# Third sums of the first chunk by accumulating transfers, wide products in the fourth f, and five smaller edits in a hybrid encoder layer

## The chip, the cores and the metric

The kernel runs on one core of one Trainium2 chip. A core has a matrix engine (TensorE, PE in the profile), a vector engine (VectorE, DVE), a scalar engine (ScalarE, ACT), a general engine (GpSimd, POOL) and a queueing engine (SyncE, SP). Each takes its instructions in order. In this kernel SP issues plain transfers and POOL issues transfers that add to what lies at their destination. The metric is device time in microseconds of one execution: 2027.13 us, the median of three runs from 2026.53 to 2027.21.

## The reference, cut to what matters

All in fp32, one layer, 512 tokens, width 2048, 44 groups ("f") of 128 hidden columns.

```python
def reference(x, ...):
    xn = rms_norm(x, attn_norm_g)
    u_val, u_gate, q, k, v = split(xn @ w_in)
    y_conv = conformer_conv(u_val, u_gate, ...)   # GLU, conv of width 31, LayerNorm over channels, swish
    y_na   = neighborhood_attention(q, k, v, rpb)
    mixed  = concat(rms_norm(y_conv, conv_out_g), rms_norm(y_na, na_out_g))
    x  = x + mixed @ w_out
    up = depthwise_conv(rms_norm(x, ffn_norm_g) @ w_up, ...)   # width 3
    gate, val = split(up)
    x  = x + (silu(gate) * val) @ w_down
    return rms_norm(x, final_norm_g)
```

## The kernel before, in words

**Weights.** Every fp32 product is three products of a faster type (fp32r). A unit of weights, 128 x 1024 values or 512 KB, is loaded by SP into one of `NR` = 7 buffers (`raw` or `ws`). `parts` (L113) lets ACT copy it to a rounded high half `whi` (L116) and lets DVE subtract that from the unit, which gives the low half `wlo` (L117). `mm3` (L124) then multiplies high by high, high by low and low by high. There are `NW` = 4 buffers of each half. `weights()` (L148) hands out the next unit of a list and asks for the units up to `AHEAD` = 3 further on, so that what makes a unit is placed some products ahead of its use.

**Order.** The code is written stage by stage. Statistics and other side work are generators that `tick` (L135) advances after a product; `tc.issue_after` lets their instructions start behind a given instruction. A scheduler then fixes one order per engine from the order written, the priorities and the buffers; instructions under `pin` keep program order.

**Stages.** First, until about 488 us, is the input projection: the convolution's columns, the values, queries and keys, with convolution, attention and their statistics between. `stats1` (L283) sums the squares of the input for the first norm, each sum a square by ACT and an addition by DVE (L170); a reduction over partitions is done by PE (L190). `group_a` (L382) computes mean and variance of the convolution's eight results `ys`: it adds them up, and one fp32 matmul with a matrix of ones (L390) sums over the channels. Then the output projection runs in two halves (`out_half`, L572), each of 16 products `po2` of which PSUM bank "mm" (three of them) takes one; `read_a` adds them to `x2` once the norm `ra` is there (L596). A bank "po" of its own serves statistics and attention.

**FFN.** Chunks of `CH` = 4 f's follow, 11 in all. For one f the up projection has four blocks of weights, A11, A21, A22 and A12, and is computed by seven products over sums of blocks. `factors(f)` (L666) makes the seven factors: c=0 is A22, c=1 is the sum A22 + A21 in the buffer `ws`, c=2 is A21 + A11 in the buffer of A21, c=3 is A11, c=4 is `ws` + A11, c=5 is A12, c=6 is `ws` + A12. For f of the first chunk `sums()` (L672) loads A22 a second time by SP into `ws` (L674) and lets POOL accumulate A21 (L675) and, into the buffer of A21, A11 (L677). The third and fourth sums, and all sums of later f's, are DVE additions (L691, L693, L698, L702). A factor's high and low halves are made from the sum, so ACT and DVE wait for it.

**Products.** `up` (L733) computes a factor's product in a "wide" form: eight matmuls of 128x512 (L743), which take high by high and high by low at once, and eight of 128x256 (L749). A factor with even c also opens the next one's bank with one wide matmul. ACT copies results from PSUM (L775) and DVE combines the seven products (L790 to L814). `up_apart` (L818) uses three matmuls of 128x256 instead (L127 to L129) and needs fewer additions (L850 to L856). `hidden` (L869) takes `up_apart` for f=3 and `up` otherwise; f=0 has its own call. `gated_tile` scales by the norm (L873, L874), convolves (L863 to L865), and multiplies (L877). From the second chunk on, the down products `pd` of the chunk before go between the up products, and POOL adds each result to the running sum in HBM (L898).

**Opening.** DVE sets a tile `warm` to one (L102), and PE multiplies it six times by itself (L231), five times 512 columns and once 256, before the first real product.

Of the kernel before, what the change touches and what calls it, by code (L numbers as in the profile page):

```python
# [31 lines left out]
NC_ = CONV // P  # L32
NP_ = HEADS // 2
NF = FF // P
U = 8
# [5 lines left out]
H = S // 2  # L41
LT = S - P
CH = 4
# [23 lines left out]
def layer(ctx: ExitStack, tc: tile.TileContext, xT, xG, xw, w_a, w_in, w_v, w_out, w_up, w_down, par, tab, g3, out, last_out):  # L67
    nc = tc.nc
# [5 lines left out]
    psm = ctx.enter_context(tc.tile_pool(name="psm", bufs=3, space=bass.MemoryType.PSUM))  # L74
    psa = ctx.enter_context(tc.tile_pool(name="psa", bufs=1, space=bass.MemoryType.PSUM))
# [9 lines left out]
    def t2(name, dt=F32):  # L85
        return tp.tile([P, S], dt, tag="t2k", name=name)

    def t4(shape, name):

        return wpool.tile(shape, F32, tag="raw", name=name, bufs=NR)  # L90

    pin = tc.keep_in_program_order
# [5 lines left out]
        o = POFF[name] + i  # L98
        return prm[:, o:o + 1]

    warm = t2("warm", F32R)
    pin(nc.vector.memset(warm.bitcast(F32), 1.0))  # L102
    ones_r = consts.tile([P, P], F32R, name="ones")
    ones = ones_r.bitcast(F32)
    nc.vector.memset(ones, 1.0)
# [3 lines left out]
    def raw_unit(src, n):  # L109
        raw = t4([P, U * P], "raw")  # L110
        return raw, nc.sync.dma_start(raw[:, :n], src)

    def parts(raw, n):  # L113
        hi = wpool.tile([P, U * P], F32R, tag="whi", name="whi", bufs=NW)
        lo = wpool.tile([P, U * P], F32R, tag="wlo", name="wlo", bufs=NW)
        i = nc.scalar.activation(hi[:, :n], raw[:, :n], AF.Copy)  # L116
        j = nc.vector.tensor_sub(lo[:, :n], raw[:, :n], hi[:, :n].bitcast(F32))  # L117
        return hi, lo, i, j

    def unit(src, n):  # L120

        return parts(raw_unit(src, n)[0], n)[:2]

    def mm3(ps, w, wk, mh, ml, start, stop):  # L124
        hi, lo = w[:2]
# [20 lines left out]
    plan, made = [], []  # L146
# [17 lines left out]
    def sum_sq(acc, src, first, to=slice(0, S)):  # L164
        if first:
            nc.scalar.activation(acc, src, AF.Square)
        else:
            q = t2("sq")[:, to]
            nc.scalar.activation(q, src, AF.Square)
            nc.vector.tensor_add(acc, acc, q)  # L170
# [45 lines left out]
    xs, x1 = [], []  # L216
    acc1 = t2("acc1")
# [9 lines left out]
    idle = consts.tile([P, 1], F32, name="idle")  # L227
    pin(nc.scalar.activation(idle, ones[:, 0:1], AF.Square))
    ps = psa.tile([P, 2, S], F32, tag="sc", name="idle")
    for n in 5 * (S,) + (H,):  # L230
        pin(nc.tensor.matmul(ps[:, 0, :n], warm[:, :P], warm[:, :n], start=True, stop=True))  # L231

    for k in range(KD):
        if k < CH:
            raw = t4([P, U * P], "raw")
            n = S + 2 * P + (0 if k else KD)
# [3 lines left out]
        else:  # L240
            if k % CH == 0:
                raw = t4([P, U * P], "raw")
            if k % CH == 0 or k == CH + 2:
                o, n = 2 * (k % CH) * P, 2 * (2 if k < 2 * CH else CH) * P
# [3 lines left out]
        h, l = t2("xh", F32R), t2("xl", F32R)  # L248
# [18 lines left out]
    for step in ORDER:  # L267
# [5 lines left out]
        i = next(a_ if step == "a" else q_)  # L273
# [9 lines left out]
    def stats1():  # L283
        yield
        for k in range(CH, KD):
            sum_sq(acc1, x1[k], False)
            if k % 4 == 3:
                yield
        for _ in range(STAT_AT):
            yield  # L290
        rstd.append((yield from rsqrt_steps(acc1, D, "rstd1", by_token=rtok)))

    steps.append(stats1())

    def project(n):
# [55 lines left out]
    ys, ypair = [], []  # L351
# [6 lines left out]
    def gated(i, pg, pv):  # L358
        g = t2("gate")
        nc.vector.tensor_mul(g, pg, rstd[0])  # L360
        nc.scalar.activation(g, g, AF.Sigmoid)
        nc.vector.tensor_mul(g, g, rstd[0])
        h = t2("ch")
        by = "p (g r c) -> p r g c"
        nc.vector.tensor_mul(h.rearrange("p (r g c) -> p r g c", r=WH, g=NG), pv.rearrange(by, r=WH, g=NG),
                             g.rearrange(by, r=WH, g=NG))
        with shifted(600):

            if i % 2 == 0:
                ypair.append(t4([P, 2, S], "y"))  # L370
            y = ypair[-1][:, i % 2]
            o = POFF["dww"] + i * CK
            nc.vector.tensor_scalar(y, h, prm[:, o + PAD:o + PAD + 1], pc("dwb", i), op0=ALU.mult, op1=ALU.add)
            for j in range(CK):
                if j != PAD:
                    a, b = max(PAD - j, 0), S + min(PAD - j, 0)
                    nc.vector.scalar_tensor_tensor(y[:, a:b], h[:, a + j - PAD:b + j - PAD], prm[:, o + j:o + j + 1],  # L377
                                                   y[:, a:b], op0=ALU.mult, op1=ALU.add)
            ys.append(y)

    ma, ra = [], []

    def group_a():
        acc = t2("acc")
        nc.vector.tensor_add(acc, ys[0], ys[1])
        for i in range(2, NC_):
            nc.vector.tensor_add(acc, acc, ys[i])
        yield
        ps = psa.tile([P, S], F32, tag="po", name="st")
        nc.tensor.matmul(ps, ones, acc, start=True, stop=True)  # L390
        mu = t2("mu")
        nc.vector.tensor_scalar(mu, ps, 1.0 / CONV, None, op0=ALU.mult)
        acc = t2("acc")
        for i in range(NC_):
            nc.vector.tensor_sub(ys[i], ys[i], mu)
            sum_sq(acc, ys[i], i == 0)
            if i == NC_ // 2 - 1:
                yield
        yield
        yield  # L400
        r = yield from rsqrt_steps(acc, CONV, "rln")
        acc = t2("acc")
        for i in range(NC_):
            nc.vector.tensor_mul(ys[i], ys[i], r)
            nc.scalar.activation(ys[i], ys[i], AF.Silu, scale=pc("lng", i), bias=pc("lnb", i))
            ma.append(split(ys[i], pc("cog", i), "ma"))
            sum_sq(acc, ys[i], i == 0)
            if i % 2:
                yield
        yield  # L410
        yield
        ra.append((yield from rsqrt_steps(acc, CONV, "ra")))
# [132 lines left out]
    p, n = -1, 0  # L545
# [26 lines left out]
    def out_half(m, read):  # L572
        for d in range(KD):
            w = weights()
            ps = psm.tile([P, S], F32, tag="mm", name="po2")
            for k in range(U):
                i = mm3(ps, w, k, m[k][0], m[k][1], k == 0, k == U - 1)
            tick(i)
            read(d, ps)
# [86 lines left out]
    def factors(f):  # L666

        def load(q):
            a[q] = raw_unit(w_up[f, q], U * P)[0]
            return a[q]  # L670

        def sums():  # L672
            a["s"] = t4([P, U * P], "ws")
            nc.sync.dma_start(a["s"], w_up[f, A22])  # L674
            nc.gpsimd.dma_start(a["s"], w_up[f, A21], accum_op=ALU.add)  # L675
            load(A21)
            nc.gpsimd.dma_start(a[A21], w_up[f, A11], accum_op=ALU.add)  # L677

        def make(c):
            if c == 0:  # L680
                load(A22)
                if f < CH:
                    sums()
                return a[A22]
            if c == 1 and f < CH:
                load(A11)
            elif c == 2 and f < CH:
                return a[A21]
            elif c == 1:
                a["s"] = t4([P, U * P], "ws")  # L690
                add(a["s"], load(A21), a[A22])  # L691
            elif c == 2:
                add(a[A21], a[A21], load(A11))  # L693
                return a[A21]
            elif c == 3:
                return a[A11]
            elif c == 4:
                add(a["s"], a["s"], a[A11])  # L698
            elif c == 5:
                return load(A12)  # L700
            else:
                add(a["s"], a["s"], a[A12])  # L702
            return a["s"]

        a = {}
        return [lambda c=c: parts(make(c), U * P)[:2] for c in range(7)]

    A11, A21, A22, A12 = range(4)
    add = nc.vector.tensor_add
# [157 lines left out]
        return y  # L867

    def hidden(f, between):  # L869
        return gated_tile(f, *(up_apart if f == CH - 1 else up)(f, between))  # L870

    def gated_tile(f, g, v):
        nc.vector.tensor_mul(g, g, rstd2[0])  # L873
        nc.vector.tensor_mul(v, v, rstd2[0])  # L874
        g, v = conv3(g, f), conv3(v, NF + f)
        nc.scalar.activation(g, g, AF.Silu)
        nc.vector.tensor_mul(g, g, v)  # L877
        return g
# [50 lines left out]
    n = CH  # L929
# [46 lines left out]
    acc = t2("acc3")  # L976
    for d in range(KD):
        ps = psm.tile([P, S], F32, tag="mm", name="pd")[:, fm]
# [8 lines left out]
    sums, v, r, y, w = (sm.tile([P, CH], F32, tag="rs" + c, name="rs" + c) for c in "lvryw")  # L987
    v, r, y, w = (t[:, :1] for t in (v, r, y, w))
# [129 lines left out]
```

## Time and profile before

| | us |
|---|---|
| median of three runs | 2027.13 |
| the profiled execution | 2026.74 |
| its span | 2024.9 |
| PE busy | 2012.7 (99%) |
| DVE busy | 1670.3 (82%) |
| ACT busy | 1051.5 (52%) |
| POOL busy | 166.5 (8%) |

In a row of a timeline the first number is the start in us from the span's beginning, the second the time, then come engine, line, operation, result, inputs and shape; "x3" means three merged instructions, and a bracket at the end says how long the engine was idle before and what ended it. The time of one matmul is longer than the distance between two, since they are pipelined; distances between starts count. In a row of windows come the bounds, the length, the busy time of PE, its weight loads, DVE, ACT and POOL, each with its instructions, and then PE's granted clock, the mean share of the 16 DMA engines, and GB/s. A row of transfers gives size and median time from issue to landing.

### The profile page before, as it was taken

The numbers are of one execution on the slowest core, as the hardware profiler recorded it, in microseconds if no ns is written. First come the engines' busy times: TensorE is split into PE (matmuls) and PEld (weight loads), VectorE is DVE, ScalarE is ACT, GpSimd is POOL, SyncE is SP. The second block draws the span as 40 slices with busy tenths as digits, with TensorE's granted clock in tenths as the row PEclk, the third lists the DMA queues.
The fourth block names the chain that finished last, engine by engine and source line by source line (L and its number), as shares of the span: only waits on it lengthen the run. The fifth ranks groups of instructions, "written<-read, shape, count | busy, mean of one in ns | idle before, by whom it ended". The sixth has DMA issues, their size and how long they took to land.

```text
span 2024.9 us, 28118 instructions
## 1 busy us (share of the span) xinstructions
PE 2012.7 (99%) x10546; PEld 1719.8 (85%) x10546; DVE 1670.3 (82%) x2302; ACT 1051.5 (52%) x1685; POOL 166.5 (8%) x196
## 2 busy tenths in 40 slices
PE   9999999999999999999999999999999999999998
PEld 7888888888888898888888888888888888888887
DVE  7986888988576899888888888888888888879875
ACT  6323344466346655555555555555555555555563
POOL 0000000000002101111111111111111111110111
PEclk9999999999999999999999999999999999999999
DMA  7232333336348745566565565565566565564683
GB/s 256 84 105 85 115 95 111 106 127 215 106 121 208 195 132 146 126 146 146 125 146 146 132 139 146 130 141 146 121 150 146 125 146 146 127 144 126 146 202 131
DMA packets 98503, 282.68 MB, mean 140 GB/s; under 512 B 10944, under 2 KB 12224, under 8 KB 98368
## 3 DMA queue, kind: packets, MB, share of 16 engines
q1 hardware_dynamic: 72000, 230.55, 37.2%
q0 software_dynamic: 26368, 50.34, 16.8%
q8 instruction: 83, 1.36, 0.3%
q14 instruction: 52, 0.43, 0.1%
HBM read 226.32 MB, written 54.53 MB: 139 GB/s over the span
## 4 chain that ended last, share of the span: by engine, by line
PE 96%; DVE 2%; DMA 1%; ACT 1%; issue 0%; SPq 0%; ACTq 0%; DVEq 0%
PE pu L743 26%; PE pu L749 14%; PE pd L129 8%; PE pd L127 8%; PE pd L128 8%; PE pj L127 5%; PE pj L129 5%; PE pj L128 5%; PE po L127 3%; PE po L128 3%; PE po L129 3%; PE pv L324 1%; PE pv L323 1%; PE pv L325 1%; PE trp L497 1%; PE po L512 1%
## 5 line engine op out<-in xcount | busy, mean ns | idle before, releaser
L116 ACT ACTIVATE whi<-raw 128x1024 fp32r<-128x1024 f32 x364 | 384.4, 1058 | 504.9 <-PE pj L128 139.7
L117 DVE TENSOR_TENSOR wlo<-raw,whi 128x1024 fp32r<-128x1024 f32 x364 | 444.8, 1223 | 211.8 <-ACT whi L116 202.9
L743 PE MATMUL pu<-xc,whi 128*128 128x512 f32 x2352 | 580.7, 391 | 0.6 <-DVE uu L797 0.3
L743 PEld LDWEIGHTS pu<-xc,whi 128*128 128x128 f32 x2352 | 433.7, 188 | 83.7 <-issue 0.7
L749 PEld LDWEIGHTS pu<-xc,wlo 128*128 128x128 f32 x2352 | 307.2, 191 | 14.7
L749 PE MATMUL pu<-xc,wlo 128*128 128x256 f32 x2352 | 311.9, 283 | 0.0
L129 PE MATMUL pd<-hh,wlo 128*128 128x512 f32 x640 | 250.7, 392 | 0.7 <-DVE wlo L117 0.7
L127 PE MATMUL pd<-hh,whi 128*128 128x512 f32 x640 | 250.1, 391 | 0.0
L128 PE MATMUL pd<-hl,whi 128*128 128x512 f32 x640 | 249.5, 390 | 0.0
L898 POOL DMA_DIRECT2D x2d<-pdc x160 | 139.3, 872 | 1119.5 <-ACT pdc L897 892.2
L127 PE MATMUL pj<-xh,whi 128*128 128x512 f32 x512 | 199.2, 394 | 0.5 <-DVE xh L253 0.5
L129 PE MATMUL pj<-xh,wlo 128*128 128x512 f32 x512 | 199.0, 391 | 0.2 <-DVE wlo L117 0.2
L128 PE MATMUL pj<-xl,whi 128*128 128x512 f32 x512 | 199.2, 392 | 0.0
L775 ACT ACTIVATE pl<-pu 128x256 f32<-128x256 f32 x294 | 109.7, 381 | 151.3 <-PE pu L743 144.3
L377 DVE SCALAR_TENSOR_TENSOR y<-ch,prm,y 128x501 f32<-128x501 f32 (+14 forms) x240 | 173.7, 743 | 4.3
L116 ACT ACTIVATE whi<-ws 128x1024 fp32r<-128x1024 f32 x132 | 139.7, 1058 | 69.7 <-PE pu L743 55.1
L117 DVE TENSOR_TENSOR wlo<-ws,whi 128x1024 fp32r<-128x1024 f32 x132 | 161.3, 1222 | 14.4 <-ACT whi L116 14.0
L129 PEld LDWEIGHTS pd<-hh,wlo 128*128 128x128 f32 x640 | 120.2, 188 | 29.6 <-DVE wlo L117 4.4
L128 PEld LDWEIGHTS pd<-hl,whi 128*128 128x128 f32 x640 | 120.3, 188 | 24.6
L127 PEld LDWEIGHTS pd<-hh,whi 128*128 128x128 f32 x640 | 120.5, 188 | 22.6
L897 ACT ACTIVATE pdc<-pd 128x512 f32<-128x512 f32 x160 | 93.9, 588 | 80.6 <-PE pd L129 67.4
L127 PEld LDWEIGHTS pj<-xh,whi 128*128 128x128 f32 x512 | 96.5, 189 | 21.2 <-ACT whi L223 1.0
(216 smaller groups left out, 2728.8 us busy)
## 6 DMA issues: line engine op xcount, KB each, us to landing
raw<-in_w_up SPq DMA_DIRECT2D x176, 512.0 KB, 3.8
raw<-in_w_down SPq DMA_DIRECT2D x88, 512.0 KB, 4.0
x2d<-pdc POOLq DMA_DIRECT2D x160, 256.0 KB, 4.9
raw<-in_w_in SPq DMA_DIRECT2D x60, 512.0 KB, 3.7
raw<-in_w_out SPq DMA_DIRECT2D x32, 512.0 KB, 3.8
raw<-in_w_v SPq DMA_DIRECT2D x16, 512.0 KB, 3.7
tab<-in_tab SPq DMA_DIRECT2D x32, 256.0 KB, 5.2
x<-in_xT SPq DMA_DIRECT2D x16, 256.0 KB, 5.5
```

Source lines behind the costliest of these rows:

```text
L116: i = nc.scalar.activation(hi[:, :n], raw[:, :n], AF.Copy)
L117: j = nc.vector.tensor_sub(lo[:, :n], raw[:, :n], hi[:, :n].bitcast(F32))
L127: nc.tensor.matmul(ps, hi[:, a], mh, start=start, stop=False)
L128: nc.tensor.matmul(ps, hi[:, a], ml, start=False, stop=False)
L129: return nc.tensor.matmul(ps, lo[:, a], mh, start=False, stop=stop)
L323: nc.tensor.matmul(ps, xh, wh[:, f], start=kk == 0, stop=False)
L377: nc.vector.scalar_tensor_tensor(y[:, a:b], h[:, a + j - PAD:b + j - PAD], prm[:, o + j:o + j + 1], y[:, a:b], op0=ALU.mult, op1=ALU.add)
L743: i = nc.tensor.matmul(ps, w[0][:, k * P:(k + 1) * P], comb[c][k], start=k == 0, stop=stop and k == ks[-1])
L749: i = nc.tensor.matmul(ps[:, H:], w[1][:, k * P:(k + 1) * P], comb[c][k][:, :H], start=False, stop=stop and k == U - 1)
L775: nc.scalar.activation(to, ps, AF.Copy)
L897: nc.scalar.activation(t, ps, AF.Copy)
L898: nc.gpsimd.dma_start(xd[d], t, accum_op=ALU.add)
```

## The change

1. The tile `warm` has 256 columns and is set by POOL; PE multiplies it 16 times with 256 columns.
2. The squares that `stats1` adds are issued behind the low half of the first unit.
3. The results `ys` are added up as each is made. `group_a` splits the sum into a high and a low half (one ACT copy, one DVE subtraction) and sums each over the channels by an fp32r matmul.
4. The product `po2` number 3 of the first half goes to the bank "po".
5. The fifth f (f=4) makes its first two sums as the first chunk does: one more load by SP, two accumulating transfers by POOL, no DVE additions L691 and L693.
6. For f=0 to 3 the third sum, `ws` + A11, is an accumulating transfer from HBM by POOL, in place of the DVE addition L698. On POOL's queue the four new transfers stand as follows: that of f=0 after the fourteenth of the sixteen L624 accumulates of the second norm; that of f=1 between L675 and L677 of f=2; that of f=2 between L675 and L677 of f=3; that of f=3 after L677 of f=3. The two of f=4 follow.
7. f=3 uses `up` instead of `up_apart`.

```diff
-    warm = t2("warm", F32R)
-    pin(nc.vector.memset(warm.bitcast(F32), 1.0))
+    warm = t2("warm", F32R)[:, :H]
+    pin(nc.gpsimd.memset(warm.bitcast(F32), 1.0))
...
-    for n in 5 * (S,) + (H,):
-        pin(nc.tensor.matmul(ps[:, 0, :n], warm[:, :P], warm[:, :n], start=True, stop=True))
+    for _ in range(16):
+        pin(nc.tensor.matmul(ps[:, 0, :H], warm[:, :P], warm, start=True, stop=True))
...
         for k in range(CH, KD):
-            sum_sq(acc1, x1[k], False)
+            with tc.issue_after(made[0][3].ins):
+                sum_sq(acc1, x1[k], False)
...
             ys.append(y)
+            if i == 1:
+                ysum.append(t2("ysum"))
+            if i:
+                nc.vector.tensor_add(ysum[0], ysum[0] if i > 1 else ys[0], y)
...
     def group_a():
-        acc = t2("acc")
-        nc.vector.tensor_add(acc, ys[0], ys[1])
-        for i in range(2, NC_):
-            nc.vector.tensor_add(acc, acc, ys[i])
+        h, l = t2("yh", F32R), t2("yl", F32R)
+        nc.scalar.activation(h, ysum[0], AF.Copy)
+        nc.vector.tensor_sub(l, ysum[0], h.bitcast(F32))
         yield
         ps = psa.tile([P, S], F32, tag="po", name="st")
-        nc.tensor.matmul(ps, ones, acc, start=True, stop=True)
+        for i, m in enumerate((h, l)):
+            nc.tensor.matmul(ps, ones_r, m, start=i == 0, stop=i == 1)
...
-            ps = psm.tile([P, S], F32, tag="mm", name="po2")
+            ps = (psa.tile([P, S], F32, tag="po", name="po2") if m is ma and d == 3 else
+                  psm.tile([P, S], F32, tag="mm", name="po2"))
...
             if c == 0:
                 load(A22)
-                if f < CH:
+                if f <= CH:
                     sums()
                 return a[A22]
-            if c == 1 and f < CH:
+            if c == 1 and f <= CH:
                 load(A11)
-            elif c == 2 and f < CH:
+            elif c == 2 and f <= CH:
                 return a[A21]
...
+            elif c == 4 and f < CH:
+                nc.gpsimd.dma_start(a["s"], w_up[f, A11], accum_op=ALU.add)
             elif c == 4:
                 add(a["s"], a["s"], a[A11])
...
     def hidden(f, between):
-        return gated_tile(f, *(up_apart if f == CH - 1 else up)(f, between))
+        return gated_tile(f, *up(f, between))
```

`unit` and `factors` also return the whole of what `parts` returns, so that the subtraction can be named in item 2.

More of the change, by code (lines that the diff above doesn't have):

```diff
@@ L120, in unit @@
     def unit(src, n):
-        return parts(raw_unit(src, n)[0], n)[:2]
+        return parts(raw_unit(src, n)[0], n)
     def mm3(ps, w, wk, mh, ml, start, stop):
@@ L379, in gated @@
             ys.append(y)
-    ma, ra = [], []
+            if i == 1:
+                ysum.append(t2("ysum"))
+            if i:
+                nc.vector.tensor_add(ysum[0], ysum[0] if i > 1 else ys[0], y)
+    ma, ra, ysum = [], [], []
     def group_a():
-        acc = t2("acc")
-        nc.vector.tensor_add(acc, ys[0], ys[1])
-        for i in range(2, NC_):
-            nc.vector.tensor_add(acc, acc, ys[i])
+        h, l = t2("yh", F32R), t2("yl", F32R)
+        nc.scalar.activation(h, ysum[0], AF.Copy)
+        nc.vector.tensor_sub(l, ysum[0], h.bitcast(F32))
         yield
         ps = psa.tile([P, S], F32, tag="po", name="st")
-        nc.tensor.matmul(ps, ones, acc, start=True, stop=True)
+        for i, m in enumerate((h, l)):
+            nc.tensor.matmul(ps, ones_r, m, start=i == 0, stop=i == 1)
         mu = t2("mu")
@@ L705, in factors @@
         a = {}
-        return [lambda c=c: parts(make(c), U * P)[:2] for c in range(7)]
+        return [lambda c=c: parts(make(c), U * P) for c in range(7)]
     A11, A21, A22, A12 = range(4)
```

## The prediction

> **What bounds the kernel now.** I read the page's chain first, then the busy time by 25 us windows, then the timeline wherever a window shows TensorE (PE) under 25.00.
>
> ```profile
> span 2024.9 us, 28118 instructions
> PE 96%; DVE 2%; DMA 1%; ACT 1%; issue 0%; SPq 0%; ACTq 0%; DVEq 0%
> ```
> ```profile
> 700.00:725.00 25.00, 24.70 (x142) 21.64 (x141) 24.72 (x37) 16.09 (x27) 1.76 (x2) 1.00 0.57 150
> 750.00:775.00 25.00, 24.26 (x133) 20.82 (x132) 24.95 (x33) 15.94 (x26) 1.76 (x2) 1.00 0.43 114
> ```
>
> PE carries the end. So a gain is either fewer PE cycles or a PE gap closed, and anything else counts only if it makes PE wait. But from 700 to 775, where most of the change lies, VectorE (DVE, the third number after the comma) is as full as PE: 24.72 and 24.95 of 25. What holds DVE up there holds PE up soon after.
>
> The profiled run took 2026.74 us, its span 2024.9, so 1.84 lies around the span. The median of the runs shown is 2027.13, 0.39 above the profiled run; I sum against 2026.74 and add 0.39. Within 0.2% is within 4.05 us of 2027.13, about what a measurement of this kernel can tell from no change.
>
> **The change part by part.**
>
> *Warm-up (memset on POOL, 16 matmuls of 256).*
>
> ```profile
> 1.45 2.72 PE L231 MATMUL idle<-warm 128*128 128x512 f32 x6 [1.45 <-DVE warm L102]
> 4.68 1.19 PE L127 MATMUL pj<-xh,whi 128*128 128x512 f32 x2 [0.51 <-DVE xh L253]
> ```
>
> The six matmuls hold 2816 columns in 2.72 us, so 4096 columns take 2.72 × 4096/2816 = 3.96 us at that rate: from 1.45 to 5.4, 0.7 past the first product's 4.68. That product waits for data, and so do those behind it, so a late start can be made up and a warmer array cannot run ahead. Between +0.7 and a gain of the 0.51 us idle I take 0. The Trainium skill ("TensorE: Matmul & The Clock Gate", Part 1) says about 3.4 us of sustained activity bring full rate; by it the longer filler could end half rate sooner, which would be worth those 0.5 us at most.
>
> *First statistics behind the first low half.*
>
> ```profile
> 25.19 2.28 DVE L170 TENSOR_TENSOR acc<-acc,sq 128x512 f32<-128x512 f32 x3
> 27.39 1.22 DVE L117 TENSOR_TENSOR wlo<-raw,whi 128x1024 fp32r<-128x1024 f32 x1
> ...
> 28.05 0.39 PE L128 MATMUL pj<-xl,whi 128*128 128x512 f32 x1
> 28.66 0.50 PE L129 MATMUL pj<-xh,wlo 128*128 128x512 f32 x1 [0.22 <-DVE wlo L117]
> ```
>
> PE's starts stand 0.61 apart where others stand 0.23 apart: 0.38 lost, because three sums go ahead of the low half (wlo). They move behind it. What is late next is the reduction L190 and the scale after it; I leave 0.1 for that. Gain 0.3 (0 to 0.4).
>
> *Mean of group A.*
>
> ```profile
> 410.46 1.02 PE L390 MATMUL st<-acc,ones 128*128 128x512 f32 x2
> ...
> 411.54 0.39 PE L129 MATMUL pj<-xh,wlo 128*128 128x512 f32 x1
> ```
>
> From 410.46 to 411.54 lie this fp32 matmul and one ordinary one (0.23): it costs 0.85. Two fp32r matmuls of 512 columns cost 2 × 0.23 = 0.45. Gain 0.4. The split adds one ACT copy and one DVE subtraction of 128x512, and seven sums move earlier, all beside projection work; bounds 0.2 to 0.5.
>
> *One output product in another bank.*
>
> ```profile
> 498.70 0.60 ACT L213 ACTIVATE ra<-st 128x512 f32<-128x512 f32 x1 [0.76 <-PE st L207]
> ...
> 499.43 0.39 PE L129 MATMUL po<-mah,wlo 128*128 128x512 f32 x1
> 500.07 0.50 PE L127 MATMUL po<-mah,whi 128*128 128x512 f32 x1 [0.26 <-DVE oa L596]
> ```
>
> PE loses 500.07 − 499.43 − 0.23 = 0.41 waiting for a bank. The "po" bank is free when ACT has read `st`, at 499.30, before it is wanted at 499.66. Gain 0.4 (0 to 0.4).
>
> *Wide products in the fourth f.*
>
> ```profile
> 730.70 0.28 PE L127 MATMUL pu<-xc,whi 128*128 128x256 f32 x1
> ...
> 750.86 2.23 PE L743 MATMUL pu<-xc,whi 128*128 128x512 f32 x9
> 752.93 2.08 PE L749 MATMUL pu<-xc,wlo 128*128 128x256 f32 x16
> 754.84 3.59 PE L743 MATMUL pu<-xc,whi 128*128 128x512 f32 x15
> ```
>
> The fourth f (f=3) holds PE from 730.70 to 750.86, 20.16 us. A wide one has 56 matmuls of 512, (752.93 − 750.86)/9 = 0.230 each, and 56 of 256, 1.91/16 = 0.119 each: 19.5 us. Gain 0.65. On DVE it adds two 128x512 and three 128x256 adds, about 2.2 us, and ACT some copies; ACT has room, DVE hardly.
>
> *Fifth f's two sums by transfers.* DVE loses L693 and L691, an add of the same shape:
>
> ```profile
> 750.39 1.22 DVE L693 TENSOR_TENSOR raw<-raw 128x1024 f32<-128x1024 f32 x1
> 759.78 1.22 DVE L117 TENSOR_TENSOR wlo<-raw,whi 128x1024 fp32r<-128x1024 f32 x1
> ...
> 759.92 0.40 PE L128 MATMUL pd<-hl,whi 128*128 128x512 f32 x1
> 761.06 0.50 PE L129 MATMUL pd<-hh,wlo 128*128 128x512 f32 x1 [0.74 <-DVE wlo L117]
> ```
>
> The 2 × 1.22 us removed about pay for the 2.2 added just before. PE's gap at 761.06 (1.14 − 0.23 = 0.91) hangs on DVE's backlog: between 0 and 0.9 I take a gain of 0.4. The two transfers and one more SP load stand behind f=3's on their queues; with f=3's 20 us of PE work over them, landing times of some 4 to 10 us (rows below) stay hidden. Without that cover each microsecond late would be one of PE's.
>
> *Third sum of the first chunk by transfers.* This decides the sign. For f < 4 the DVE add L698 (`ws += A11`) becomes a POOL accumulate from HBM. POOL issues in order, and for f=1 the new transfer stands behind L675 of f=2 (689.79) and ahead of L677 (691.73).
>
> ```profile
> 689.79 0.90 POOL L675 DMA_DIRECT2D ws<-in_w_up  x1 [17.80 <-DMA ws<-in_w_up]
> 691.73 0.89 POOL L677 DMA_DIRECT2D raw<-in_w_up  x1 [1.04 <-DVE rsy L176]
> ```
> ```profile
> DMA to landing us min/median/max: 5.6/7.2/7.5
> ...
> DMA to landing us min/median/max: 6.2/8.0/10.2
> ```
> ```profile
> raw<-in_w_up SPq DMA_DIRECT2D x176, 512.0 KB, 3.8
> ```
> ```profile
> 699.00:700.00 1.00, 1.00 (x9) 0.92 (x8) 0.69 (x2) 0.47 (x2) 0.00 (x0) 1.00 1.04 279
> ```
> ```profile
> 693.47 1.23 DVE L117 TENSOR_TENSOR wlo<-ws,whi 128x1024 fp32r<-128x1024 f32 x1
> 694.61 1.13 DVE L201 SCALAR_TENSOR_TENSOR dg<-ident,rsy,dg 128x128 fp32r<-128x128 f32 x4
> ...
> 696.32 1.22 DVE L702 TENSOR_TENSOR ws<-ws,raw 128x1024 f32<-128x1024 f32 x1
> ...
> 699.59 1.22 DVE L117 TENSOR_TENSOR wlo<-ws,whi 128x1024 fp32r<-128x1024 f32 x1 [0.31 <-PE pu L749]
> ...
> 702.30 0.75 DVE L864 SCALAR_TENSOR_TENSOR uy<-g,prm,uy 128x511 f32<-128x511 f32 x1 [0.28 <-ACT uy L863]
> ...
> 705.00 0.42 DVE L797 TENSOR_TENSOR uu<-pu,pl 128x256 f32<-128x256 f32 x1
> ...
> 708.37 1.22 DVE L117 TENSOR_TENSOR wlo<-ws,whi 128x1024 fp32r<-128x1024 f32 x1
> ...
> 715.52 1.22 DVE L698 TENSOR_TENSOR ws<-ws,raw 128x1024 f32<-128x1024 f32 x1
> ```
> ```profile
> 705.56 0.47 PE L743 MATMUL pu<-xc,whi 128*128 128x512 f32 x1 [0.30 <-DVE uu L797]
> ```
>
> It is issued at 689.79 + 0.90 = 690.7. The landing times are those of L675 (5.6 to 7.5), of L677 (6.2 to 10.2) and of a plain load of the same size (3.8); the DMA engines are full here (share 1.04). The 10.2 belongs to the transfer issued at 691.73, second behind L675, the nearest row: the new one takes its place. Landing 690.7 + 10.2 = 700.9.
>
> Behind it wait ACT's high half (1.06) and then DVE's low half (693.47 today), in order. Between that low half's start and L797's lie 705.00 − 693.47 = 11.53 us; 1.71 of it (694.61 to 696.32) now goes ahead and about 0.75 is idle time around the marked waits. So L797 starts 11.53 − 1.71 − 0.75 = 9.05 after the low half, which is landing + 1.06 + 9.05. It frees the bank PE waits for at 705.56, already late by 0.30 today. PE's delay is therefore landing + 10.1 − 705.0 = landing − 694.9: 6.0 at 700.9; 1.4 at the fastest accumulate (5.6); none at 3.8 (694.5); 7.5 if it shares the full engines with the transfer behind it.
>
> The Trainium skill ("DMA: Bandwidth & Descriptors", Anatomy of one DMA) puts such a transfer at 2.0 us plus bytes at 436 GB/s, an estimate of 3.2 us here: landing 693.9 and no delay, though the accumulates measured here took twice that or more.
>
> For f=2 the new transfer is issued when DVE has done the low half of 708.37, at 709.6. At 5.6 to 7.5 us it lands at 715.2 to 717.1, is split by ACT until 716.3 to 718.2, and DVE, there at 715.52, idles 0.8 to 2.7 but saves the 1.14 of L698: −0.3 to +1.6. f=3 is alike. Together I take a loss of 0.3, bounds 0 and 3.2. For f=0 the new transfer follows this one on POOL, and its sum is first read here:
>
> ```profile
> 664.36 0.86 POOL L624 DMA_DIRECT2D sq<-sq  x1 [1.24 <-ACT xc L610]
> ```
> ```profile
> 677.13 1.06 ACT L116 ACTIVATE whi<-ws 128x1024 fp32r<-128x1024 f32 x1 [1.79 <-PE pu L128]
> ```
>
> From 665.2 to 677.1 are 11.9 us, over the longest 10.2: nothing. It delays the last two sums of squares of the second norm behind it on POOL's queue, by no more than half its own time on full engines, about 2 us; DVE's idle time in front of that norm may take that in, so 0 to 2, and I take 0.
>
> *Sum.* Gains 0.3 + 0.4 + 0.4 + 0.65 + 0.4 = 2.15; losses 6.0 + 0.3 = 6.3. Net +4.15: 2026.74 + 4.15 + 0.39 = 2031.3. The 10.2 us is the longest of eight such landings, so I shade it by 0.3 and say 2031.0, 0.19% over the median: nominally no change, on its slow edge.
>
> **Rivals.**
>
> *The transfers are hidden.* If f=1's new accumulate lands as a plain load does, by 694.5, nothing waits and the gains stay: 2027.13 − 2.15 = 2025.0. For it: 3.8 us for the same bytes, and L675's smallest 5.6 leaves only 1.4. Against: the full engines after 693, and no accumulate under 5.6. It decides if the landing takes under 4.2 us. Chance 0.20.
>
> *The later f's wait too.* If f=2 and f=3 land like L677's worst, at 10.2 us, each holds DVE up by 709.6 + 10.2 + 1.06 − 715.52 − 1.14 = 4.2 us (nothing up to a landing time of 6.0, then one for one), in a stretch where DVE has nothing to spare: one such adds 4 to the forecast, 2035; both 2039. This is the one that ends on the other side of the bound. For it: DVE at 24.95 of 25 and the wide f=3 adding 2.2. Against: fewer loads run beside them. Chance 0.25.
>
> *The statistics of the second norm come late*, pushed by f=0's transfer: 2 us more, 2033. Chance 0.05.
>
> *More is gained than named*, DVE being freed at the right moments by 4 × 1.14: all gains at their upper bounds with the opening's 0.5 give 0.4 + 0.5 + 0.4 + 0.65 + 0.9 + 0.5 = 3.35, 2023.8, and 2022.7 with L698's 1.14 once more. Chance 0.05.
>
> **How the numbers follow.** My forecast has 0.45, with its own range 2028 to 2033; about 0.25 of it lies within 0.2% and 0.20 above. Hidden: 0.17 within, 0.03 below. The two slower rivals are above, the last below. Faster 0.08, same 0.42, slower 0.50. The range goes from 2024 (hidden, with a little more gained) to 2036 (one later f waiting in full).
>
> **What would show it.** Right: DVE and ACT idle some 6 us before f=1's fifth halves, ended by a DMA into `ws`, and one PE gap of 5 to 7 us shortly after 705; no PE gap at 28.7, 500.1; two short matmuls for `st` near 410; f=3 in 19.5 us. Wrong: that transfer landing under 5 us, or gaps of the same kind at f=2 and f=3, or a PE gap before the first wide product.

## The result and the profile after

The changed kernel takes 2041.77 us (median of six, 2038.56 to 2043.21) against 2026.65 us before (median of six, 2026.3 to 2027.21): ratio 1.0073, 95% interval 1.0062 to 1.0084. It is slower by 15 us, where 2031.0 with a range to 2036 was forecast. The profiled execution took 2043.18 us, near the top of its runs.

The page of the changed kernel, its first lines and its chain:

```profile
span 2041.3 us, 28049 instructions
PE 2018.6 (99%) x10500; PEld 1720.2 (84%) x10500; DVE 1666.2 (82%) x2301; ACT 1052.6 (52%) x1692; POOL 172.0 (8%) x203
...
PE 95%; DVE 2%; DMA 1%; issue 1%; ACT 1%; ACTq 0%; POOL 0%; DVEq 0%; POOLq 0%
```

```profile
75.00:100.00 25.00, 25.00 (x112) 20.72 (x111) 24.86 (x36) 9.88 (x14) 0.00 (x0) 1.00 0.22 64
```
```profile
75.00:100.00 25.00, 22.81 (x95) 18.41 (x95) 24.96 (x35) 8.80 (x12) 0.00 (x0) 0.94 0.28 85
...
700.00:725.00 25.00, 17.40 (x79) 14.68 (x78) 16.42 (x23) 11.56 (x17) 2.62 (x3) 0.80 0.69 165
750.00:775.00 25.00, 23.34 (x131) 19.68 (x129) 23.63 (x33) 16.45 (x26) 0.00 (x0) 1.00 0.59 168
```

The page as a whole hardly differs; the windows show where the time goes. The single row above is the stretch from 75 to 100 in the kernel before, the others are the changed kernel; the rows of before from 700 and from 750 stand at the head of the prediction. PE, the first number after the comma, falls to 17.40 of 25 in the stretch from 700, and to 22.81 in the stretch from 75, where it was full before. In both of these the granted clock (third number from the end) drops too: 0.80 and 0.94. In 700 to 725 DVE falls to 16.42, so PE and DVE wait together.

Line numbers from here on are those of the kernel at hand. In the changed kernel L681 and L683 are the accumulates that were L675 and L677, L704 is the new transfer, L751 and L757 are the wide product's L743 and L749, L783 is the copy L775, and L805 is the addition L797.

The starts of the same matmuls in both timelines give the bill:

| start of | before | after | shift |
|---|---|---|---|
| first `pv`, value projection | 51.53 | 50.81 | −0.72 |
| first `sc`, attention | 236.58 | 239.95 | +3.37 |
| last `pj` of the input projection | 477.35 | 480.25 | +2.90 |
| first `pu`, up projection | 669.14 | 671.54 | +2.40 |
| first `pd`, down products | 759.22 | 773.99 | +14.77 |
| end of the span | 2024.9 | 2041.3 | +16.4 |

Two places lose: 4.1 us at the value projection and 12.4 us in the first chunk, with 1.6 more just behind it.

*The value projection.* Timelines of ACT and PE, first before, then after:

```profile
89.59 1.06 ACT L116 ACTIVATE whi<-raw 128x1024 fp32r<-128x1024 f32 x1 [4.38 <-PE pv L324]
93.21 0.69 ACT L333 ACTIVATE vg<-pv,rsy 128x512 f32<-128x512 f32 x1 [2.56 <-PE pv L325]
...
95.05 0.39 PE L127 MATMUL pj<-xh,whi 128*128 128x512 f32 x1
```
```profile
94.30 1.06 ACT L116 ACTIVATE whi<-raw 128x1024 fp32r<-128x1024 f32 x1 [4.38 <-PE pv L325]
95.27 0.67 ACT L334 ACTIVATE vg<-pv,rsy 128x512 f32<-128x512 f32 x1
95.95 0.68 ACT L337 ACTIVATE vx<-pv,rsy 64x512 f32<-64x512 f32 x1
...
94.11 0.39 PE L326 MATMUL pv<-wlo,xh 128*128 128x512 f32 x1
96.68 0.50 PE L127 MATMUL pj<-xh,whi 128*128 128x512 f32 x1 [2.19 <-ACT vx L337]
...
97.70 0.63 PE L127 MATMUL pj<-xh,whi 128*128 128x512 f32 x1
98.13 0.63 PE L128 MATMUL pj<-xl,whi 128*128 128x512 f32 x1
```

PE's next product needs a bank that ACT frees by `vg` and `vx`. Before, ACT did that at 93.21. After, the high half at 94.30 stands ahead of `vg` in ACT's order; it waits for its own buffer, which the last `pv` products hold until then, and the copies wait behind it. PE stands 2.35 us beyond its pace and then starts matmuls 0.43 apart in place of 0.23 for some 3.4 us; the granted clock is 0.50 between 98 and 100.

*The first chunk, f=1.* POOL's queue, the landing times of the new transfers (L704), ACT, DVE and PE of the changed kernel, with one row of DVE in the kernel before (680.50):

```profile
694.53 0.88 POOL L681 DMA_DIRECT2D ws<-in_w_up  x1 [20.17 <-DMA ws<-in_w_up]
695.16 1.17 POOL L704 DMA_DIRECT2D ws<-in_w_up  x1
```
```profile
DMA to landing us min/median/max: 7.1/7.8/10.5
```
```profile
705.78 1.06 ACT L116 ACTIVATE whi<-ws 128x1024 fp32r<-128x1024 f32 x1 [8.72 <-DMA ws<-in_w_up]
706.74 0.36 ACT L783 ACTIVATE vv<-pu 128x256 f32<-128x256 f32 x1
```
```profile
680.50 0.69 DVE L661 TENSOR_TENSOR acc<-acc,sq 128x512 f32<-128x512 f32 x1
```
```profile
685.61 0.69 DVE L667 TENSOR_TENSOR acc<-acc,sq 128x512 f32<-128x512 f32 x1 [2.63 <-DMA sq<-sq]
...
706.87 1.23 DVE L117 TENSOR_TENSOR wlo<-ws,whi 128x1024 fp32r<-128x1024 f32 x1 [7.96 <-ACT whi L116]
...
716.44 0.42 DVE L805 TENSOR_TENSOR uu<-pu,pl 128x256 f32<-128x256 f32 x1
```
```profile
706.89 2.69 PE L751 MATMUL pu<-xc,whi 128*128 128x512 f32 x8 [1.88 <-ACT whi L116]
709.37 1.91 PE L757 MATMUL pu<-xc,wlo 128*128 128x256 f32 x8
717.00 0.77 PE L751 MATMUL pu<-xc,whi 128*128 128x512 f32 x1 [5.72 <-DVE uu L805]
717.57 1.91 PE L757 MATMUL pu<-xc,wlo 128*128 128x256 f32 x8
719.27 4.12 PE L751 MATMUL pu<-xc,whi 128*128 128x512 f32 x12
```

The transfer is issued behind L681, at 695.16, and lands 10.5 us later, at 705.7. ACT waits 8.72 for it, DVE 7.96, and PE stops twice, by 2.0 and 6.0 us beyond its pace: first for the high half itself, then for the bank that L805 frees. The granted clock is 0.50 from about 715 to 721. Eight 128x256 matmuls then take 1.70 (717.57 to 719.27), against 0.95 at full rate. The row at 685.61 is a second finding: DVE waits 2.63 us for the last sum of squares of the second norm, on which it did not wait before (680.50).

*In f=3 and behind it* (in f=2 PE has no gap of note):

```profile
750.17 1.06 ACT L116 ACTIVATE whi<-ws 128x1024 fp32r<-128x1024 f32 x1 [4.26 <-PE pu L751]
...
751.26 1.22 DVE L117 TENSOR_TENSOR wlo<-ws,whi 128x1024 fp32r<-128x1024 f32 x1 [2.88 <-ACT whi L116]
```
```profile
753.23 0.50 PE L751 MATMUL pu<-xc,whi 128*128 128x512 f32 x1 [1.28 <-ACT pl L783]
...
775.48 0.50 PE L128 MATMUL pd<-hl,whi 128*128 128x512 f32 x1 [0.86 <-DVE hl L891]
...
777.82 0.50 PE L128 MATMUL pd<-hl,whi 128*128 128x512 f32 x1 [0.68 <-DVE hl L891]
```

f=3's transfer was issued at 743.01 and landed at 750.07. The bracket of ACT's row at 750.17 names PE, but the products that held that buffer of `whi` were done at about 746.4; what came at 750.07 is the landing. ACT and DVE stand for it, PE follows with a gap of 1.4, since ACT's copies out of PSUM queue behind the waiting high half, and DVE's lost time comes up again at the first down products, 1.03 + 0.85 beyond pace.

### The profile page after: what moved, and what is told of

Its sections match the earlier page's. It is cut to its first block, busy times and chain, and to the rows that moved or that the text cites. A ratio compares the mean times of both kernels' runs of the same rounds, so it can differ in the third digit from the quotient of the medians.

```text
span 2041.3 us, 28049 instructions
## 1 busy us (share of the span) xinstructions
PE 2018.6 (99%) x10500; PEld 1720.2 (84%) x10500; DVE 1666.2 (82%) x2301; ACT 1052.6 (52%) x1692; POOL 172.0 (8%) x203
## 4 chain that ended last, share of the span: by engine, by line
PE 95%; DVE 2%; DMA 1%; issue 1%; ACT 1%; ACTq 0%; POOL 0%; DVEq 0%; POOLq 0%
PE pu L751 26%; PE pu L757 14%; PE pd L129 8%; PE pd L128 8%; PE pd L127 8%; PE pj L127 6%; PE pj L129 5%; PE pj L128 5%; PE po L127 3%; PE po L128 3%; PE po L129 3%; PE pv L325 1%; PE pv L324 1%; PE pv L326 1%; PE trp L502 1%
## 5 line engine op out<-in xcount | busy, mean ns | idle before, releaser
L117 DVE TENSOR_TENSOR wlo<-raw,whi 128x1024 fp32r<-128x1024 f32 x364 | 444.2, 1221 | 210.7 <-ACT whi L116 203.8
L751 PE MATMUL pu<-xc,whi 128*128 128x512 f32 x2408 | 596.8, 392 | 8.9 <-DVE uu L805 5.7
L751 PEld LDWEIGHTS pu<-xc,whi 128*128 128x128 f32 x2408 | 444.8, 189 | 96.1 <-issue 6.2
L757 PEld LDWEIGHTS pu<-xc,wlo 128*128 128x128 f32 x2408 | 316.1, 192 | 15.1
L757 PE MATMUL pu<-xc,wlo 128*128 128x256 f32 x2408 | 320.7, 283 | 0.0
L128 PE MATMUL pd<-hl,whi 128*128 128x512 f32 x640 | 249.6, 390 | 1.6 <-DVE hl L891 1.5
L129 PE MATMUL pd<-hh,wlo 128*128 128x512 f32 x640 | 250.3, 391 | 0.0
L129 PE MATMUL pj<-xh,wlo 128*128 128x512 f32 x512 | 199.2, 392 | 0.0
L128 PE MATMUL pj<-xl,whi 128*128 128x512 f32 x512 | 198.8, 391 | 0.0
L783 ACT ACTIVATE pl<-pu 128x256 f32<-128x256 f32 x301 | 112.2, 381 | 154.9 <-PE pu L751 147.9
L117 DVE TENSOR_TENSOR wlo<-ws,whi 128x1024 fp32r<-128x1024 f32 x132 | 161.1, 1220 | 27.9 <-ACT whi L116 27.7
L378 DVE SCALAR_TENSOR_TENSOR y<-ch,prm,y 128x500 f32<-128x500 f32 (+14 forms) x240 | 173.5, 740 | 4.3
L129 PEld LDWEIGHTS pd<-hh,wlo 128*128 128x128 f32 x640 | 120.1, 188 | 28.4 <-DVE wlo L117 3.2
L128 PEld LDWEIGHTS pd<-hl,whi 128*128 128x128 f32 x640 | 120.2, 188 | 27.5 <-DVE hl L891 2.9
```

Of the source, the lines that this page charges most:

```text
L128: nc.tensor.matmul(ps, hi[:, a], ml, start=False, stop=False)
L129: return nc.tensor.matmul(ps, lo[:, a], mh, start=False, stop=stop)
L751: i = nc.tensor.matmul(ps, w[0][:, k * P:(k + 1) * P], comb[c][k], start=k == 0, stop=stop and k == ks[-1])
L757: i = nc.tensor.matmul(ps[:, H:], w[1][:, k * P:(k + 1) * P], comb[c][k][:, :H], start=False, stop=stop and k == U - 1)
L783: nc.scalar.activation(to, ps, AF.Copy)
```

## The experiments

Each group of four kernels was timed beside runs of the kernel before: 2026.77 us with the first four, 2027.0 with the next, 2027.09 with the last.

**Third sums by VectorE again.**

```diff
-            elif c == 4 and f < CH:
-                nc.gpsimd.dma_start(a["s"], w_up[f, A11], accum_op=ALU.add)
```

> The changed kernel with the third sum of f=0 to 3 added by VectorE again; everything else of the change stays. Theory A (the new accumulating transfers stop PE in f=1, through the high and low half that wait for the landing): the two gaps of 2.0 and 6.0 us in f=1, the slow clock after them and the 1.4 us gap in f=3 go, some 12 us in all: 2041.8 - 12 = 2030 (2028 to 2032). Rival B (VectorE, loaded by the wide fourth f, is what runs late, and the transfers only show it): VectorE gets 4.6 us more work in the same stretch, so the gaps stay or grow: 2040 or more.

Measured 2027.79 (2026.48 to 2028.49), ratio 1.0001 (0.9993 to 1.0010). Theory A, and more of it than expected: 14.0 us off the changed kernel. Both gaps of f=1, the one in f=3 and those at the down products are gone. The gap at 94 is still there, but this execution shows no slow clock behind it (granted clock 1.00):

```profile
94.03 0.39 PE L326 MATMUL pv<-wlo,xh 128*128 128x512 f32 x1
96.61 0.50 PE L127 MATMUL pj<-xh,whi 128*128 128x512 f32 x1 [2.19 <-ACT vx L337]
96.95 0.39 PE L128 MATMUL pj<-xl,whi 128*128 128x512 f32 x1
97.18 0.40 PE L129 MATMUL pj<-xh,wlo 128*128 128x512 f32 x1
```

The same gap costs 2.5 us here and 4.1 in the other trace. So a stop may or may not take the clock down, and that is one likely cause of the spread of the runs: 2.0 us in this kernel and 0.7 in the version below that has no gap at 94.

**Mean of group A as before.** The seven sums stand in `group_a` again, with one fp32 matmul.

```diff
-            if i == 1:
-                ysum.append(t2("ysum"))
-            if i:
-                nc.vector.tensor_add(ysum[0], ysum[0] if i > 1 else ys[0], y)
...
-        for i, m in enumerate((h, l)):
-            nc.tensor.matmul(ps, ones_r, m, start=i == 0, stop=i == 1)
+        nc.tensor.matmul(ps, ones, acc, start=True, stop=True)
```

> The changed kernel with the mean of group A as before (the seven sums in group_a, one fp32 matmul). Theory A (the seven sums placed early change ACT's order: one more high half goes ahead of the copies that free the value projection's banks, and PE stands 2.35 us and then runs some 3.4 us at half rate): the gap at 94 goes, 4.1 us gained and 0.45 lost at the fp32 matmul: 2041.8 - 3.6 = 2038.2 (2037 to 2039.5). Rival B (the statistics that are put off behind the first low half are what comes late there): the gap stays, 2042.2.

Measured 2038.48 (2037.6 to 2040.78), theory A: no gap at 94, although the first statistics are still put off. The split is undone here too, but the fourth experiment keeps the split and has no gap at 94 either. What moved the high half ahead on ACT is thus the place of seven sums on DVE: with them early, the scheduler that fixes one order per engine chose another order for ACT.

**Third sums by transfers alone, in the kernel before.**

```diff
+            elif c == 4 and f < CH:
+                nc.gpsimd.dma_start(a["s"], w_up[f, A11], accum_op=ALU.add)
             elif c == 4:
```

> The kernel before with one edit alone: the third sum of f=0 to 3 by accumulating transfers. Theory A (this edit alone makes the stop): 2026.7 + 12 = 2038.5 (2036 to 2040.5), with gaps of about 2 and 6 us in f=1. Rival B (it costs what was forecast, 6.3, and the rest of the 12 comes from its meeting with the other edits): 2033.

Measured 2038.25 (2036.67 to 2040.45), 11.5 over the kernel before: theory A. This edit makes the stop without the others' help, and the 6.3 of losses in the forecast were little more than half of it.

**Without both.** The third sums by VectorE, and the split kept while the sums stand where they stood before.

```diff
-            if i == 1:
-                ysum.append(t2("ysum"))
-            if i:
-                nc.vector.tensor_add(ysum[0], ysum[0] if i > 1 else ys[0], y)
...
+        ysum.append(t2("ysum"))
+        nc.vector.tensor_add(ysum[0], ys[0], ys[1])
+        for i in range(2, NC_):
+            nc.vector.tensor_add(ysum[0], ysum[0], ys[i])
         h, l = t2("yh", F32R), t2("yl", F32R)
```

> The changed kernel with the third sums by VectorE again and, for the mean of group A, the split into two fp32r matmuls kept but the seven sums added where they stood before. Theory A (those two places are the whole loss, the other edits gain what their terms say): no gap at 94 nor in f=1; 2041.8 - 12 - 4.1 = 2025.7 (2024.3 to 2027). Rival B (the fifth f's sums and the wide fourth f only move VectorE's backlog to the down products, 1.9 us lost there now against 0.9 before): 2026.5 to 2028, no better than before.

Measured 2030.16 (2028.79 to 2032.43): a miss for both theories. The gap at 94 is gone and the down products show none, but new waits came, in a place neither had named (waits of PE from 420 to 520):

```profile
PE st L190 <- DVE acc L170: 2.1, 2, 1.5
PE st L207 <- ACT ao L523: 1.4, 1, 1.4
PE po L127 <- ACT ra L213: 0.7, 1, 0.7
```

The variance and the attention's norm come late. The seven sums and the split then both stand between the last `y` and the mean. Against the version below that has the late sums without the split (2024.62), the mean comes at 412.54 in place of 411.19, and the last of the eight subtractions of the mean at 431.38 in place of 427.81, with attention work of DVE ahead of it. That this order makes the norms late is a reading of the traces; no run puts the order alone right. The split, then, wants the early sums; what is bad about them is what they do to ACT's order at 94.

**f=1 alone by VectorE.**

```diff
-            elif c == 4 and f < CH:
+            elif c == 4 and f < CH and f != 1:
```

> The changed kernel with the third sum of f=1 alone added by VectorE; those of f=0, 2 and 3 stay accumulating transfers. Theory A (f=1 is special: its transfer goes out between two others of POOL while the DMA engines are full): both gaps of f=1 and the slow clock after them go, about 9.7 us, and the others stay small: 2041.8 - 9.7 = 2032 (2030.5 to 2034). Rival B (any such transfer comes late, the next one then makes the stop): f=2 stops PE by 4 us or more, 2036 or above.

Measured 2034.47 (2032.81 to 2035.93), 7.3 off the changed kernel. That is 0.5 above theory A's range. f=1 is the largest part, but the other three still cost 2034.47 − 2027.79 = 6.7, more than theory A left them. It isn't rival B's stop either: PE loses 0.4 in f=2. The rest is a gap in f=1, which has no transfer of its own now, and the down products again (the last row, 0.3, is there before the change too):

```profile
PE pu L751 <- ACT pl L783: 2.0, 2, 1.8
PE pd L128 <- DVE hl L891: 1.5, 2, 0.9
PE pu L751 <- DVE uu L805: 0.3, 1, 0.3
```

**POOL's queue turned round.** The new transfer of f=1 goes out ahead of the first accumulate of f=2. The same edit names f=4, where it changes nothing: f=3's transfer already stood first there. `third` lists the new transfers.

```diff
-            nc.gpsimd.dma_start(a["s"], w_up[f, A21], accum_op=ALU.add)
+            with tc.issue_after(third[-1].ins) if f in (2, 4) else nullcontext():
+                nc.gpsimd.dma_start(a["s"], w_up[f, A21], accum_op=ALU.add)
...
-                nc.gpsimd.dma_start(a["s"], w_up[f, A11], accum_op=ALU.add)
+                third.append(nc.gpsimd.dma_start(a["s"], w_up[f, A11], accum_op=ALU.add))
```

> The changed kernel with the order of POOL's queue turned round: the new transfer of f=1 is issued before the first accumulate of f=2 (and that of f=3 before those of f=4). Theory A (it is late because it stands behind the other one, first on the queue and then on the DMA engines): it is issued some 1.5 us earlier and lands 5 to 7.5 us after that, near 700 in place of 705.7; PE's stop shrinks by 5 to 7 us: 2035.5 (2034 to 2037.5), while f=2's own sums land later. Rival B (the DMA engines are full anyhow and it lands after 10 us whatever its place): over 2039.

Measured 2035.7 (2032.67 to 2038.12), theory A. Here L707 is the new transfer and L684 the accumulate:

```profile
694.63 0.88 POOL L707 DMA_DIRECT2D ws<-in_w_up  x1 [20.17 <-DVE rsr L174]
695.19 1.23 POOL L684 DMA_DIRECT2D ws<-in_w_up  x1
...
702.73 1.06 ACT L116 ACTIVATE whi<-ws 128x1024 fp32r<-128x1024 f32 x1 [7.81 <-DMA ws<-in_w_up]
```

Issued only 0.5 us earlier, it lands 3.1 us earlier, 8.0 after issue (702.6) in place of 10.5. So its place behind the other accumulate costs 3.1 us of landing time in these two executions, and 6.1 of the run time with what hangs on it; but first in the queue it is still too slow for a use that leaves 4.2: PE's longest stop in f=1 is now 3.0 us.

**Mean and third sums both undone.** The edits of the first two experiments together.

> The changed kernel with the third sums by VectorE and the mean of group A as before, sums and fp32 matmul. Theory A: against the version with the third sums alone undone (2027.8) the gap at 94 goes (4.0 with its slow clock) and the fp32 matmul and the gap before the variance come back (0.45 + 0.3): 2024.5 (2023.8 to 2025.5). Rival B (as with the sums moved back but the split kept, 2030.2, the late statistics take the gain again): 2028 or more.

Measured 2024.62 (2024.4 to 2025.82), ratio 0.9989 (0.9980 to 0.9997): theory A. What is left of the change gains 2.4 us.

**Banks read first.** The sums stay early; the first high half after the first half of the value projection is held behind the copies `vg` and `vx` on ACT. Third sums by VectorE.

```diff
+    hold = []
...
+        if hold:
+            with tc.issue_after(hold.pop().ins):
+                i = nc.scalar.activation(hi[:, :n], raw[:, :n], AF.Copy)
...
+        if half == 0:
+            hold.append(last)
```

Here `last` is the last `vx` copy.

> The changed kernel with the third sums by VectorE and one high half (the first after the first half of the value projection) held back on ACT until the copies that free the value projection's banks are done; the sums stay where the change puts them. Theory A (only that order makes the gap at 94): gap gone, the rest as in the version with the third sums alone undone: 2027.8 - 4.0 = 2023.8 (2023 to 2024.8). Rival B (the high half that is held back is then late itself): a gap of 1 us or more right after the value projection, 2025 or above.

Measured 2024.04 (2023.84 to 2024.56), ratio 0.9985 (0.9976 to 0.9994): theory A, and the fastest version. `vg` starts at 92.74 and the gap at 94 is gone. That one order on ACT was worth 2027.79 − 2024.04 = 3.75 us (4.0 when each is taken against the runs of the kernel before beside it).

**Only f=1 by transfer.**

```diff
-            elif c == 4 and f < CH:
+            elif c == 4 and f == 1:
```

> The changed kernel with the third sum by transfer for f=1 alone; f=0, 2 and 3 by VectorE. Theory A (the four transfers' costs add up: f=1 is worth the 7.3 by which its removal made the changed kernel faster): 2027.8 + 7.3 = 2035.1 (2034 to 2036.3). Rival B (the stop of f=1 covers part of what f=0 costs, so alone it costs more): 2037 or above. Rival C (it costs what was forecast, 6.0 or less, because without the transfer of f=0 the chain of the norm is on time): 2033.8 or below.

Measured 2037.03 (2034.97 to 2039.33): 9.2 over 2027.79, just inside rival B. Its transfer is issued at 694.42 and lands after 11.0 us. Alone it costs more than the 7.3 that its removal gave, so it hides part of another's cost. PE's waits from 680 to 800, in its longest execution:

```profile
PE pu L751 <- DVE uu L805: 7.1, 1, 7.1
PE pu L751 <- ACT whi L116: 2.2, 1, 2.2
```

The down products do not wait here, so that wait belongs to f=2's and f=3's transfers. No run has one of those two alone.

**Only f=0 by transfer.**

```diff
-            elif c == 4 and f < CH:
+            elif c == 4 and f == 0:
```

> The changed kernel with the third sum by transfer for f=0 alone. Theory A (it pushes the last sum of squares of the second norm, VectorE waits 2 us for that, and PE stands for some 2 us in f=1, with a slow clock after it): 2027.8 + 2.5 = 2030.3 (2029.3 to 2031.5). Rival B (VectorE has idle time there that takes it in, as the prediction had it): 2028 (2027 to 2028.8).

Measured 2029.11 (2026.6 to 2032.54): 1.3 over 2027.79, short of theory A's range by 0.2 and beyond rival B's by 0.3, with a wide spread. The mechanism is A's: the wait of 1.8 below is also the one that was left in f=1 when its own transfer was taken out (2.0 above). In the profiled execution, the longest, DVE and PE read:

```profile
686.24 0.69 DVE L667 TENSOR_TENSOR acc<-acc,sq 128x512 f32<-128x512 f32 x1 [3.26 <-DMA sq<-sq]
```
```profile
PE pu L751 <- ACT pl L783: 1.8, 1, 1.8
PE st L190 <- DVE acc L667: 0.9, 1, 0.9
PE pu L751 <- DVE uu L805: 0.3, 1, 0.3
```

**The best version without the wide fourth f,** and **the best version without the fifth f's transfers.**

```diff
-        return gated_tile(f, *up(f, between))
+        return gated_tile(f, *(up_apart if f == CH - 1 else up)(f, between))
```

> The best version so far (third sums by VectorE, value projection's banks read first) with f=3 as before, three 128x256 matmuls. Theory A (the wide form is worth its PE time, 0.65): 2024.0 + 0.65 = 2024.7. Rival B (the 2.2 us that it adds on VectorE come back as a gap, so it is worth nothing): 2024.0 or less.

Measured 2024.23 (2023.98 to 2024.84), so the wide form is worth about 0.2, nearer to rival B; its runs overlap those of the best version.

```diff
-                if f <= CH:
+                if f < CH:
```

(and the two other conditions alike.)

> The best version so far with the fifth f's first two sums by VectorE again. Theory A (they free VectorE where it is full; without them the gap before the first down products comes back, and more of it, since the wide fourth f has loaded VectorE): a gap of 0.9 to 2 us there, 2024.0 + 1.4 = 2025.4 (2024.9 to 2026.2). Rival B (VectorE has caught up by then): 2024.0 (2023.7 to 2024.4).

Measured 2028.02 (2026.42 to 2029.61): the transfers of the fifth f are worth 4.0, well over theory A. PE's waits from 740 to 800, none of which the best version has (L134 and L135 are L128 and L129 of before, L123 is L117, and L897 makes `hl`, the low half of what the down products multiply):

```profile
PE pd L135 <- DVE wlo L123: 1.6, 1, 1.6
PE pd L134 <- DVE hl L897: 0.8, 1, 0.8
```

Beyond pace these are 1.8 and 1.0, and some seven matmuls 0.43 apart follow. The likely reading is that the two edits belong together: the wide fourth f overloads DVE just where the fifth f's transfers relieve it. No run takes both out of the best version; the kernel before, which has neither, shows a gap of 0.91 there.

## Why the prediction was wrong

The forecast missed by 2041.8 − 2031.0 = 10.8 us. The single steps below that were missing or too small come to 3.75 for the order on ACT, 3.2 for f=1, 1.3 for f=0 and 3.2 for f=2 and f=3, together 11.45; the gains came out 0.85 larger than forecast, which leaves 10.6. (The part of f=2 and f=3 is a remainder, so the sum closes in part by construction.)

*Mean of group A: the step that failed outright.* The prediction put the seven early sums down as lying "beside projection work" and counted the matmul's 0.4. The matmul is right: the two fp32r matmuls start at 412.98 and 413.21, 0.23 apart, and from before to after this stretch gains 0.47. But the sums changed ACT's order at 94, shown by undoing them (no gap) and by restoring the order alone (3.75 us). No rival had it.

*Third sum of f=1: mechanism and place right, size too small.* The landing time was forecast as 10.2 and measured 10.5; that ACT and then DVE wait, and that PE stops at the bank L797 (now L805) frees, came as written. The formula gives L805 at landing + 10.1, 715.8; it was 716.44. Two things made it larger. First, the transfer was issued at 695.16, where 690.7 + 2.4 of earlier shift is 693.1: 2 us later, as DVE's wait at 685.61 put off what frees the buffer `ws` for f=2's load, which POOL's queue waits for first. f=0's transfer is only a part of that: with f=1's transfer alone DVE still waits 0.81 there, and the transfer goes out some 1.2 us late. Second, a stop of this length takes the clock down, which the sum had at nothing: some 2 us after 717. PE also stopped a time that the prediction had not named, at 706.89, for the high half itself; that stop lies inside the delay the formula gives, so it adds nothing of its own. Forecast 6.0; alone it measures 9.2.

*Third sum of f=0: taken as 0, bound 2.* Its own landing is hidden, as written; the delay of the norm's last sum of squares isn't absorbed: DVE waits 2.63 us for it, and 1.2 to 3.3 in the traces of all versions with this transfer, against 0 to 0.9 in those without. Alone 1.3 us. It was a rival with a chance of 0.05.

*Third sums of f=2 and f=3: taken as 0.3, bound 3.2.* By the four transfers' 14.0 less f=1's 9.2 and f=0's 1.3, 3.5 are left for them and for what the four do together; the trace shows 1.4 in f=3 and 1.9 at the down products. The rival "later f's wait too" had this mechanism, with a landing of 10.2 us and a loss of 4.2 for each. The landings were shorter: DVE waits 1.18 us for f=2's transfer (at 730.02) and 2.88 for f=3's. How much of the 3.5 each has stays open.

*Fifth f's sums: gain 0.4 forecast, 4.0 measured beside the wide fourth f; the wide fourth f: 0.65 forecast, about 0.2 measured.* The prediction did say that the 2.4 us removed pay for the 2.2 added; it priced what remains of the gap and not what the fourth f would cost without the relief.

*What held.* First statistics: no gap at 28 any more, gain near 0.38. Output product in another bank: the gap at 499 is gone. Warm-up: 0 taken, the first `pv` is 0.72 earlier, of which 0.38 is that gap, so some 0.3 is the opening's, inside the bounds. It shows at the first two real products: the row behind them starts 1.0 us after theirs before (4.68 to 5.67) and 0.7 after (4.69 to 5.39), so PE leaves its slow pace sooner. The gains were forecast as 2.15 and are 3.0 in the best version.

*Small slips in its working, on which nothing rests.* 11.53 − 1.71 − 0.75 is 9.07 and not 9.05. The fastest accumulate of before, 5.6 us, is 1.75 times the 3.2 and not twice. The 7.5 given for a transfer that shares the engines comes with no working.

## What to carry to other kernels

On an engine that works in order, a wait for a slow transfer is paid by everything queued behind it, so taking 1.2 us off a vector engine by putting a 10 us transfer ahead of it pays only where the use is further off than the slowest landing seen. Moving work that is itself hidden can still reorder another engine when a scheduler fixes the orders: compare the order of every engine around the places where a buffer or bank must be freed. Two edits that load and relieve the same engine in the same stretch should be priced as one.

## What the runs showed of the hardware

A stop of PE can cost more than its own length: after 2.35 us of standing still, some eight matmuls followed at 0.43 us each (granted clock 0.50) in one execution, and none in another of the same code at that place, so that the same gap cost 4.1 us in one and 2.5 in the other. The Trainium skill ("TensorE: Matmul & The Clock Gate", Part 1) says the activity window is free-running, so that the point of change varies; that agrees with these two traces, which do not show the cause. Shorter stops than that were followed by a slow clock too: in the run with f=0's transfer alone, PE stood 2.0 us beyond its pace and the nine matmuls behind took 3.72 us in place of 2.07 (granted clock 0.50 from 702 to 704). After stops of 5.6 to 7.1 us it was so in all four traces that have one (the changed kernel, the third sums alone, the mean of group A as before, only f=1): the eight 128x256 matmuls behind took 1.70 or 1.71.

The four new transfers of 512 KB took 7.1 to 10.5 us from issue to landing in the changed kernel, and all of its fourteen accumulating transfers of that size 7.1 to 11.8, where plain loads of that size took 3.8 by the median before. The estimate of 3.2 us by the page "DMA: Bandwidth & Descriptors" of the Trainium skill, Anatomy of one DMA, does not hold for them here, where other transfers run beside them.
